# Two loads moved to another queue, copies given a priority, transposes spread and a split begun earlier in a fused hybrid layer

## The chip, the core and the metric

One NeuronCore of a Trainium2 chip runs the whole kernel. TensorE (PE) multiplies matrices into the eight banks of PSUM, VectorE (DVE) and ScalarE (ACT) work elementwise and empty PSUM, GpSimd (POOL) does a little elementwise work and issues some transfers, and SyncE (SP) issues most of the transfers. Each engine, and each queue of transfers, works off its own list of instructions strictly in order: an instruction that waits holds up everything behind it on that engine. The metric is the device time of one execution in microseconds, and less is better.

## The reference, cut to what matters

```python
h = rmsnorm(x) * gain                      # (512, 2048), all in float32
u = h @ w_in                               # 4104 + 4288 + 2 * 2048 columns
u_fox, u_rwkv, g_a, g_b = split(u)
o_a = fox_attention(q, k, v, log_f) * silu(z_a)      # 8 heads of 128
o_b = (groupnorm(rwkv7_scan(...)) + bonus) * silu(z_b)   # 16 heads of 64
m = sigmoid(g_a) * (o_a @ w_proj_fox) + sigmoid(g_b) * (o_b @ w_proj_rwkv)
return rmsnorm(x + m @ w_out) * final_gain
```

The two gates g_a and g_b are products of the normalised input (512 x 2048) with 2048 x 2048 weights each. The merge needs both gates, both branch outputs and the projections.

## The kernel before

**Numbers as pairs.** Every large product is taken in three float32r products: an operand a is split into hi (rounded to float32r) and lo = a - hi, and hi*hi, hi*lo and lo*hi are added in PSUM. So each piece of weights that arrives (`raw`) costs ACT one copy (`whi`, line 267) and DVE one subtraction (`wlo`, line 268) before PE can use it. `next_piece` keeps up to four raw pieces in flight on SP's queue (line 240); a new one can only be issued when `wlo` of an old one is done. It splits pieces up to three ahead, with a priority of 150 (`HW`).

**Who orders what.** The order on PE and SP is the order of the program (`manual_schedule`). ACT, DVE and POOL get their order from a planner that goes by priority and by the times that it expects; `tc.high_priority(offset=...)` raises a priority, 300 for `HP`, 150 for `HW`. The order is fixed before the run.

**Stage 1** (to about 950 us) interleaves the input products of the two branches with the attention heads and the recurrence (`rwkv_front`, `rwkv_back`, `rwkv_chain`). The chain's small copies between its products carry `HP`. The last chain ends with the store of its output to `ob_d` in POOL's queue (line 771).

**The gates** are four half-width products, g = 0 to 3, each taken in seven block products instead of eight (a Strassen scheme). The first of the seven, called c11, is done for all g in a loop of its own (line 1041): 96 products of 128x512 into two PSUM banks for each g, in two halves kb = 0 and 1. After kb = 0 both banks are copied out (`p1`, line 1060) and stored to `p1_d`; after kb = 1 their tanh is taken (line 1064) and stored to `sg_d`. The next half goes into the same banks.

While c11 runs, DVE and ACT build sums of the blocks of the normalised input (`sum_step`: three DVE operations and one ACT copy each, for "d1", "s3", "s2" and "s4", four times each). "d1" lies in the tiles named by eight tags of the attention (`fqh` to `fpT0`), "s2" is wanted by units 6, and "s4" by units 3.

When the last chain is done, `open_late` gives the memory of the recurrence to `gates_rest`, which does the other six products as units (g, p, j): for g = 0 units 5 and 7 alternate for j = 0 to 3, then come four units 6, four units 3 and four units 4. Each unit is 12 PE products. Unit 5 loads weight blocks b11 and b12 and adds them (`X`), unit 7 loads b22 and makes two sums more, unit 6 works on what is left in `X`, and unit 3 on b22 as it is; unit 4 takes `X` after a transfer in POOL's queue has added the missing block to it (line 969). `load(upto)` issues the loads of 512 KB in SP's queue (line 949), one or more units ahead; `prep(n)` makes a unit's operands. At unit (5, 0) of each g the two `p1` tiles are read back (line 991).

**The projections and the merge.** After the gates `branch(0, ob_d)` loads the eight tiles of the recurrence's output and splits them, the first four into the tags of "d1" (line 1099). Two branches (br) by four column blocks (n) by eight pieces (k) of 12 products follow, each n in four banks. In br = 1 the merged tile of block n - 1 is transposed by PE after k = 4 (`turn_merged`, line 1109): four groups of four 128x128 transposes, each group into one bank, emptied by ACT (`mhi`) and DVE (`mlo`). The last of the four comes in the output product, before its ninth piece (kk = 8). The output product then runs to the end.

Of the kernel before, what the change touches and what calls it, by code (L numbers as in the profile page):

```python
# [9 lines left out]
F32 = mybir.dt.float32  # L10
F32R = mybir.dt.float32r
# [6 lines left out]
P = 128  # L18
# [38 lines left out]
def hybrid_layer(  # L57
# [363 lines left out]
    def split(hi, lo, a):  # L421

        S.copy(hi, a)  # L423
        V.tensor_tensor(lo, a, hi.bitcast(F32), ALU.subtract)  # L424
# [430 lines left out]
    def stage1():  # L855
# [40 lines left out]
            return a[:, KB * kb + 2 * j:KB * kb + 2 * j + 2, 256 * th:256 * th + 256]  # L896

        d1 = []

        def sum_step(which, j):  # L900
            two = lambda nm: fox.tile([P, T], F32, tag="fpr", bufs=2, name=f"{nm}_{which}_{j}").rearrange(
                "p (k t) -> p k t", k=2)
            if which == "d1":
                tags = ("fqh", "fql", "fkh", "fkl", "fv", "fz", "fcb", "fpT0")[2 * j:2 * j + 2]
                d1.append([fox.tile([P, T], F32R, tag=t, name=f"d1_{t}").rearrange("p (k t) -> p k t", k=2)
                           for t in tags])
            hl = (hhi, hlo)
            a11, a21, a12, a22 = ([quarter(a, kb, th, j) for a in hl] for kb in range(2) for th in range(2))
            x, y, op, dst = {"d1": (a21, a22, ALU.subtract, d1[j]), "s3": (a11, a21, ALU.subtract, a21),
                             "s2": (d1[j], a11, ALU.subtract, a11), "s4": (a12, a11, ALU.add, a12)}[which]  # L910
            st, su = two("st"), two("su")
            tt(V, st, x[0].bitcast(F32), y[0].bitcast(F32), op)
            tt(V, su, x[1].bitcast(F32), y[1].bitcast(F32), op)
            tt(V, st, st, su, ALU.add)
            split(dst[0], dst[1], st)
# [18 lines left out]
        def gates_rest(wp):  # L934
# [8 lines left out]
            def load(upto):  # L943
                while at[0] < len(loads) and loads[at[0]][0] <= upto:
                    n, b = loads[at[0]]
                    at[0] += 1
                    g, p, j = units[n]
                    t = wp.tile([P, 2, 512], F32, tag=f"b{b}", bufs=3 if b == "22" else 2, name=f"b{b}_{g}{p}{j}")
                    nc.sync.dma_start(t, gate_w(g, int(b[0]) - 1, int(b[1]) - 1, j).rearrange("(k p) m -> p k m", p=P))
                    raw[n, b] = t  # L950

            def prep(n):
# [31 lines left out]
            for n, (g, p, j) in enumerate(units):  # L984
                ready_upto(n + 2)
                load(n + 4)
                if (p, j) == ("5", 0):
                    pz = [ps_mm(f"z5_{g}_{t}") for t in range(2)]
                    p1 = [ev("p1", f"p1_{g}_{t}") for t in range(2)]
                    for t in range(2):  # L990
                        nc.sync.dma_start(p1[t], p1_d[g, t])
                elif (p, j) == ("7", 0):
                    if g % 2:
                        px = [ps_ms(f"x7_{g}"), ps_y(f"y7_{g}")]
                    else:
                        px = [psm.tile([P, T], F32, tag="ch", bufs=2, name=f"x7_{g}_{t}") for t in range(2)]
                elif (p, j) == ("6", 0):
                    py = [ps_ms(f"y6_{g}_{t}") for t in range(2)]
                ps = pz if p in "53" else px if p in "74" else py
                hi, lo = ready.pop(n)  # L1000
                begin, end = p in "576", p in "634"
                for t in range(2):
                    for kk in range(2):
                        k = 2 * j + kk
                        th, kb = {"7": (1, 0), "6": (0, 0), "3": (0, 1), "4": (1, 1)}.get(p, (0, 0))
                        if p == "5":
                            ah, al = (a[:, kk, t * P:(t + 1) * P] for a in d1[j])
                        else:
                            ts = slice(256 * th + t * P, 256 * th + (t + 1) * P)
                            ah, al = (a[:, KB * kb + k, ts] for a in (hhi, hlo))  # L1010
                        for a, w, i in ((ah, hi, 0), (ah, lo, 1), (al, hi, 2)):
                            mm(ps[t], a, w[:, kk, :], start=begin and k == 0 and i == 0,
                               stop=end and k == KB - 1 and i == 2, skip_group_check=True)
                            yield
                    if j < 3:
                        continue
                    if p == "5":
                        p5 = [None, None] if t == 0 else p5
                        p5[t] = ev("p5", f"p5_{g}_{t}")
                        S.copy(p5[t], ps[t])  # L1020
                    elif p == "6":
                        tt(V, p1[t], p1[t], py[t], ALU.add)
                        u3 = ev("u3", f"u3_{g}_{t}")
                        tt(V, u3, p1[t], px[t], ALU.add)
                        tt(V, p5[t], p5[t], u3, ALU.subtract)
                        S.activation(p5[t], p5[t], AF.Tanh, scale=0.5)
                        store_gate(p5[t], g, 1, 1, t)
                    elif p == "3":
                        u3 = ev("u3", f"c12_{g}_{t}")
                        tt(V, u3, pz[t], p1[t], ALU.subtract)  # L1030
                        S.activation(u3, u3, AF.Tanh, scale=0.5)
                        store_gate(u3, g, 0, 1, t)
                    elif p == "4":
                        tt(V, p1[t], p1[t], px[t], ALU.add)
                        S.activation(p1[t], p1[t], AF.Tanh, scale=0.5)
                        store_gate(p1[t], g, 1, 0, t)
                if left and p == "6":
                    sum_step(*left.pop(0))

        rest = []  # L1040
        for g in range(4):
            ps = [ps_mm(f"c11_{g}_{t}") for t in range(2)]
            for kb in range(2):
                for j in range(4):
                    ws = [next_piece(), next_piece()]
                    order = [(kk, t) for kk in range(2) for t in range(2)]
                    if j == 3:
                        order = [(kk, t) for t in range(2) for kk in range(2)]
                    for kk, t in order:
                        k = 2 * j + kk  # L1050
                        ah, al = (a[:, KB * kb + k, t * P:(t + 1) * P] for a in (hhi, hlo))
                        whi, wlo = (w[:, 0, :] for w in ws[kk])
                        for a, w, i in ((ah, whi, 0), (ah, wlo, 1), (al, whi, 2)):
                            mm(ps[t], a, w, start=kb == 0 and k == 0 and i == 0,
                               stop=kb == 1 and k == KB - 1 and i == 2, skip_group_check=True)
                            yield
                        if j == 3 and kk == 1:
                            if kb == 0:
                                p1 = keep.tile([P, T], F32, tag=KEEP[t], name=f"p1_{g}_{t}")
                                S.copy(p1, ps[t])  # L1060
                                G.dma_start(p1_d[g, t], p1)
                            else:
                                sg = keep.tile([P, T], F32, tag=KEEP[2 + t], name=f"c11_{g}_{t}")
                                S.activation(sg, ps[t], AF.Tanh, scale=0.5)
                                store_gate(sg, g, 0, 0, t)
                    if free["fox"] == 7 and first_sums:
                        sum_step(*first_sums.pop(0))
                    if g == 3 and kb == 1 and not first_sums:
                        sum_step("s2", j)
                    open_late()  # L1070
# [16 lines left out]
                nc.sync.dma_start(sg, sg_d[br][t * P:(t + 1) * P, n * 512:(n + 1) * 512])  # L1087
                sgs[br, n, t] = sg

        FT = ("fqh", "fql", "fkh", "fkl", "fv", "fz", "fcb", "fpT0")  # L1090

        def branch(br, src):

            got = []
            for i in range(8):
                o = mg.tile([P, T], F32, tag="oraw", bufs=4, name=f"oraw_{br}_{i}")
                nc.sync.dma_start(o, src[i])
                if i // 4 == br:
# [32 lines left out]
        for br in range(2):  # L1131
            for n in range(4):
                load_gates(br, n)
                pss = four_banks(n, f"p_{br}_{n}")
                for k in range(KB):
                    whi, wlo = next_piece()
                    ohi, olo = both[br][k]
                    for t in range(4):
# [4 lines left out]
                        yield  # L1143
                        mm(pss[t], olo[:, ts], whi[:, 0, :], start=False, stop=(k == KB - 1))
                        yield
                    if br == 1 and n > 0 and k == 4:
                        yield from turn_merged(n - 1)
                    if br == 0 and n == 3 and k == 3:
                        both.append(branch(1, oa_d))
                for t in range(4):  # L1150
# [54 lines left out]
    for n in range(4):  # L1205
        pss = four_banks(n, f"o_{n}")
        for kk in range(KC if n < 3 else KC // 2):
            whi, wlo = next_piece()
            if n == 0 and kk == 8:
                for _ in turn_merged(3):  # L1210
                    pass
            if n == 1 and kk % 2 == 0:
                load_late(KC // 2 + kk // 2)
            for t in range(4):
# [54 lines left out]
```

## Time and profile before

| what | value |
|---|---|
| runs | 1679.1, 1683.52, 1687.18 us; median 1683.52 us |
| the profiled execution | 1678.78 us, of which the span of the trace is 1677.0 us |
| PE busy | 1600.5 us, 95% of the span |
| DVE, ACT, POOL busy | 1128.4 us (67%), 772.5 us (46%), 127.5 us (8%) |
| transfers | 216.39 MB, mean 129 GB/s |
| granted TensorE clock, mean | 0.988 |

The shares of busy time are means over stages; a stage is read from the tables of windows and from the waits. Sums are made against the profiled execution; the median of the runs shown is 4.7 us above it.

### The profile page before, as it was taken

The page shows a single profiled execution, that of the slowest core. Times are in us where ns is not written, and L with a number is a line of the kernel's source. Part 1 is how long each engine was busy: PE and PEld are TensorE (multiplying, and loading weights), DVE is VectorE, ACT ScalarE, POOL GpSimd, SP SyncE. Part 2 cuts the span into 40 slices and gives each one's busy share as a digit, 9 for nine tenths or more (in the row PEclk, how much of TensorE's full clock was granted, in tenths as well). Part 3 has the DMA queues.
Part 4 walks back from the last instruction along what each step waited for, and adds up shares of the span by engine and source line. Part 5 has one row for each costly group of instructions (what it writes and reads, how often), then busy time and mean ns, then how long its engine had stood idle before and what let it go on. Part 6 is the DMA issues. An engine that isn't in the chain of part 4 may idle for free. (4 is left out here: it accounts for less than half of the span.)

```text
span 1677.0 us, 23568 instructions
## 1 busy us (share of the span) xinstructions
PE 1600.5 (95%) x8378; PEld 1303.1 (78%) x8378; DVE 1128.4 (67%) x2173; ACT 772.5 (46%) x1503; POOL 127.5 (8%) x205
## 2 busy tenths in 40 slices
PE   6999899999999999999999898699999999999998
PEld 5888687787787877877878777488888788778886
DVE  6468677786697687776976779977886334544432
ACT  7533545536436446464464376444444322323322
POOL 3000000000000001000010000011111000001110
PEclk9999999999999999999999999799999999999999
DMA  5343234243333342433333467678775545363422
GB/s 166 97 104 93 75 79 111 64 117 86 89 92 95 88 105 76 104 86 92 87 92 94 115 190 218 200 220 218 231 230 149 189 154 171 128 206 127 138 83 100
DMA packets 235756, 216.39 MB, mean 129 GB/s; under 512 B 40326, under 2 KB 174062, under 8 KB 234998
## 3 DMA queue, kind: packets, MB, share of 16 engines
q1 hardware_dynamic: 224582, 183.40, 38.7%
q0 software_dynamic: 9616, 28.34, 6.2%
q10 hardware_dynamic: 1440, 3.15, 0.5%
q8 instruction: 66, 1.08, 0.3%
q14 instruction: 52, 0.43, 0.1%
HBM read 193.84 MB, written 20.99 MB: 128 GB/s over the span
## 5 line engine op out<-in xcount | busy, mean ns | idle before, releaser
L136 PE MATMUL p<-whi_p,o 128*128 128x512 f32 x512 | 161.0, 394 | 2.8 <-ACT o L423 1.9
L136 PEld LDWEIGHTS p<-whi_p,o 128*128 128x128 f32 x512 | 96.1, 188 | 25.6 <-ACT o L423 2.4
L482 DVE TENSOR_TENSOR Wt<-W,Lt 128x16 f32<-128x16 f32 (+30 forms) x248 | 101.6, 410 | 6.2
L268 DVE TENSOR_TENSOR wlo_p<-raw_p,whi_p 128x512 fp32r<-128x512 f32 x64 | 43.5, 691 | 88.6 <-ACT whi_p L267 88.6
L136 PE MATMUL p<-wlo_p,o 128*128 128x512 f32 x256 | 100.8, 394 | 0.4 <-DVE wlo_p L268 0.2
L268 DVE TENSOR_TENSOR wlo_o<-raw_o,whi_o 128x512 fp32r<-128x512 f32 x56 | 42.6, 762 | 81.4 <-ACT whi_o L267 81.1
L267 ACT ACTIVATE whi_p<-raw_p 128x512 fp32r<-128x512 f32 x64 | 40.5, 632 | 115.3 <-PE p L136 42.2
L136 PE MATMUL o<-whi_o,mhi 128*128 128x512 f32 x224 | 87.2, 389 | 0.0
L136 PE MATMUL o<-whi_o,mlo 128*128 128x512 f32 x224 | 87.2, 389 | 0.0
L136 PE MATMUL o<-wlo_o,mhi 128*128 128x512 f32 x224 | 87.2, 389 | 0.0
L423 ACT CAST h<-X 128x1024 fp32r<-128x1024 f32 x48 | 50.5, 1053 | 69.9 <-PE z L136 25.3
L136 PE MATMUL c<-whi_g,hhi 128*128 128x512 f32 x128 | 53.4, 418 | 25.4 <-ACT whi_g L267 16.8
L424 DVE TENSOR_TENSOR l<-X,h 128x1024 fp32r<-128x1024 f32 x48 | 58.7, 1222 | 26.7 <-ACT h L423 26.4
L267 ACT ACTIVATE whi_o<-raw_o 128x512 fp32r<-128x512 f32 x56 | 35.4, 631 | 89.5 <-PE o L136 80.6
L642 DVE TENSOR_REDUCE W<-Wt 128x8 f32<-128x16 f32 (+30 forms) x248 | 72.6, 293 | 5.6
L136 PEld LDWEIGHTS p<-wlo_p,o 128*128 128x128 f32 x256 | 48.1, 188 | 12.2 <-DVE wlo_p L268 1.5
L719 ACT ACTIVATE pre<-SV,E 64x64 f32<-64x64 f32 x112 | 38.6, 345 | 41.0 <-DVE SV L732 40.1
L267 ACT ACTIVATE whi_g<-raw_g 128x512 fp32r<-128x512 f32 x64 | 39.7, 630 | 33.8 <-PE c L136 16.1
L423 ACT CAST h<-b 128x1024 fp32r<-128x1024 f32 x32 | 33.7, 1052 | 46.7 <-PE y L136 24.3
L136 PE MATMUL c<-wlo_g,hhi 128*128 128x512 f32 x128 | 52.5, 410 | 0.8 <-DVE wlo_g L268 0.8
L136 PE MATMUL u_fq<-hhi,whi_fq 128*128 128x512 f32 x128 | 52.4, 409 | 0.0
L136 PE MATMUL u_fq<-hlo,whi_fq 128*128 128x512 f32 x128 | 52.4, 409 | 0.0
(426 smaller groups left out, 4692.5 us busy)
## 6 DMA issues: line engine op xcount, KB each, us to landing
b<-in_w_in_dram SPq DMA_DIRECT2D x64, 512.0 KB
raw_g<-in_w_in_dram SPq DMA_DIRECT2D x64, 256.0 KB
raw_o<-in_w_out_dram SPq DMA_DIRECT2D x56, 256.0 KB
raw_k<-in_w_in_dram SPq DMA_DIRECT2D x32, 256.0 KB
raw_r<-in_w_in_dram SPq DMA_DIRECT2D x32, 256.0 KB
raw_z<-in_w_in_dram SPq DMA_DIRECT2D x32, 256.0 KB
raw_v<-in_w_in_dram SPq DMA_DIRECT2D x32, 256.0 KB
raw_fq<-in_w_in_dram SPq DMA_DIRECT2D x32, 256.0 KB
```

Source lines behind the costliest of these rows:

```text
L136: PE.matmul(out, lhsT=lhsT, rhs=rhs, start=start, stop=stop, **kw)
L267: S.activation(whi, raw, AF.Copy)
L268: V.tensor_tensor(wlo, raw, whi.bitcast(F32), ALU.subtract)
L423: S.copy(hi, a)
L424: V.tensor_tensor(lo, a, hi.bitcast(F32), ALU.subtract)
L482: eng.tensor_tensor(o, a, b, op)
L642: V.tensor_reduce(W[:, :, i], tmp[:, :, 0:i + 1], AX.X, ALU.add)
L719: S.activation(pre[hs[q]], SV[hs[q], c, q, :], AF.Copy, scale=E1[hs[q], c, CH:CH + 1])
```

## The change

1. The first loads of `gates_rest` (units n < 4, six loads of 512 KB) and the two `p1` loads of g = 0 are issued in POOL's queue instead of SP's.
2. The copies and tanh between c11's halves get the priority of the recurrence's chain (`HP`).
3. `turn_merged` is taken one group of four transposes at a time: after k = 3, 4, 5 and 6 in the projections, before kk = 7, 8, 9 and 10 in the output product, instead of four groups at once.
4. The first four tiles of the recurrence's output are loaded and split during the last gates' units (g = 3, units 3 and 4, j = 0 and 2), not after them. Their raw tiles come from the attention's tag `fpr`.

```diff
+        FT = ("fqh", "fql", "fkh", "fkl", "fv", "fz", "fcb", "fpT0")
+        o_first = []
+        def split_o(i, br, src):
+            o = fox.tile([P, T], F32, tag="fpr", bufs=2, name=f"oraw_{br}_{i}")
+            nc.sync.dma_start(o, src[i])
+            hi, lo = (fox.tile([P, T], F32R, tag=FT[2 * i + x], name=f"o{x}_{br}_{i}") for x in range(2))
+            split(hi, lo, o)
+            o_first.append((hi, lo))
...
-                    nc.sync.dma_start(t, gate_w(g, int(b[0]) - 1, int(b[1]) - 1, j).rearrange("(k p) m -> p k m", p=P))
+                    (G if n < 4 else nc.sync).dma_start(
+                        t, gate_w(g, int(b[0]) - 1, int(b[1]) - 1, j).rearrange("(k p) m -> p k m", p=P))
...
-                        nc.sync.dma_start(p1[t], p1_d[g, t])
+                        (G if g == 0 else nc.sync).dma_start(p1[t], p1_d[g, t])
...
+                if g == 3 and p in "34" and j % 2 == 0:
+                    split_o(len(o_first), 0, ob_d)
...
-                                S.copy(p1, ps[t])
+                                with tc.high_priority(offset=HP):
+                                    S.copy(p1, ps[t])
...
-                                S.activation(sg, ps[t], AF.Tanh, scale=0.5)
+                                with tc.high_priority(offset=HP):
+                                    S.activation(sg, ps[t], AF.Tanh, scale=0.5)
...
-            got = []
-            for i in range(8):
+            got = o_first if br == 0 else []
+            for i in range(len(got), 8):
...
-                    if br == 1 and n > 0 and k == 4:
-                        yield from turn_merged(n - 1)
+                    if br == 1 and n > 0 and 2 < k < 7:
+                        if k == 3:
+                            turning = turn_merged(n - 1)
+                        next(turning)
...
-            if n == 0 and kk == 8:
-                for _ in turn_merged(3):
-                    pass
+            if n == 0 and 6 < kk < 11:
+                if kk == 7:
+                    turning = turn_merged(3)
+                next(turning)
```

## Rows read from the trace of the kernel before

**Rows 1.** The page's head: the span, and PE's busy time and instructions.
```profile
span 1677.0 us, 23568 instructions
PE 1600.5 (95%) x8378; PEld 1303.1 (78%) x8378; DVE 1128.4 (67%) x2173; ACT 772.5 (46%) x1503; POOL 127.5 (8%) x205
```

**Rows 2.** PE's waits, whole run: who waited for whom, total us, times, longest.
```profile
PE c L136 <- ACT whi_g L267: 16.8, 2, 15.8
...
PE mT L140 <- DVE mlo L1121: 4.5, 4, 1.7
...
PE z L136 <- DVE l L424: 2.7, 1, 2.7
PE c L136 <- ACT p L1060: 2.4, 3, 1.0
PE p L136 <- ACT o L423: 1.9, 1, 1.9
...
PE c L136 <- ACT c L1064: 1.2, 2, 0.7
...
PE p L136 <- ACT whi_p L267: 0.9, 1, 0.9
```

**Rows 3.** Stages of 20 us: length, busy us by engine, PEclk, DMA share, GB/s.
```profile
1040.00:1060.00 20.00, 4.24 (x20) 3.19 (x18) 18.75 (x27) 7.27 (x11) 1.62 (x3) 0.70 0.25 91
1060.00:1080.00 20.00, 18.94 (x73) 14.77 (x73) 16.99 (x25) 11.22 (x18) 1.08 (x2) 0.88 0.71 221
1080.00:1100.00 20.00, 17.29 (x63) 13.73 (x64) 18.93 (x18) 7.90 (x9) 0.02 (x1) 0.83 0.74 252
```

**Rows 4.** PE in order of time: start, us, [idle before and its releaser].
```profile
1043.74 0.39 PE L136 MATMUL c<-whi_g,hlo 128*128 128x512 f32 x1
1059.90 0.79 PE L136 MATMUL c<-whi_g,hhi 128*128 128x512 f32 x1 [15.76 <-ACT whi_g L267]
...
1063.53 0.63 PE L136 MATMUL c<-whi_g,hhi 128*128 128x512 f32 x1
1063.95 0.63 PE L136 MATMUL c<-wlo_g,hhi 128*128 128x512 f32 x1
```

**Rows 5.** ACT in order of time around the end of PE's longest wait.
```profile
1058.27 1.04 ACT L423 CAST h<-X 128x1024 fp32r<-128x1024 f32 x1 [4.12 <-DVE X L482]
1059.22 0.62 ACT L267 ACTIVATE whi_g<-raw_g 128x512 fp32r<-128x512 f32 x1
```

**Rows 6.** SP's queue in order of time, from several windows.
```profile
1039.72 0.92 SPq L240 DMA_DIRECT2D raw_g<-in_w_in_dram  x2
...
1061.20 2.06 SPq L240 DMA_DIRECT2D raw_g<-in_w_in_dram  x2
...
1071.09 0.93 SPq L949 DMA_DIRECT2D b<-in_w_in_dram  x2
```

**Rows 7.** DVE in order of time: a sum for units 3, two sums of weights.
```profile
1053.52 0.69 DVE L482 TENSOR_TENSOR st_s<-hhi 128x512 f32<-128x512 f32 x1
...
1056.96 1.22 DVE L482 TENSOR_TENSOR X<-b,b 128x1024 f32<-128x1024 f32 x1
...
1080.75 1.23 DVE L482 TENSOR_TENSOR b<-b,b 128x1024 f32<-128x1024 f32 x1 [1.33 <-DMA b<-in_w_in_dram]
```

**Rows 8.** The chain that ended last: start, us, what.
```profile
1072.07 8.59 DMA b<-in_w_in_dram
...
1113.33 10.99 PE z L136 x48
```

**Rows 9.** POOL in order of time, and the issues of line 969 (KB, us to landing).
```profile
1049.63 0.54 POOL L771 DMA_DIRECT2D ob_d<-y  x1 [4.03 <-DVE y L770]
...
1099.98 1.28 POOL L969 DMA_DIRECT2D X<-in_w_in_dram  x1 [24.59 <-DVE l L424]
...
X<-in_w_in_dram POOLq DMA_DIRECT2D x16, 512.0 KB, 6.2
```

**Rows 10.** PE and ACT at one boundary between c11's halves.
```profile
988.54 0.50 PE L136 MATMUL c<-whi_g,hhi 128*128 128x512 f32 x1 [0.93 <-ACT p L1060]
...
1044.17 0.58 ACT L1060 COPY p<-c 128x512 f32<-128x512 f32 x1 [0.77 <-PE c L136]
```

**Rows 11.** SP's queue at the start of the projections.
```profile
1302.75 2.13 SPq L1097 DMA_DIRECT2D oraw<-ob_d  x4
1304.92 2.04 SPq L1087 DMA_DIRECT2D sg<-sg_d  x4
1307.01 3.09 SPq L240 DMA_DIRECT2D raw_p<-in_w_proj_rwkv_dram  x3
```

More of the change, by code (lines that the diff above doesn't have):

```diff
@@ L903, in sum_step @@
             if which == "d1":
-                tags = ("fqh", "fql", "fkh", "fkl", "fv", "fz", "fcb", "fpT0")[2 * j:2 * j + 2]
+                tags = FT[2 * j:2 * j + 2]
                 d1.append([fox.tile([P, T], F32R, tag=t, name=f"d1_{t}").rearrange("p (k t) -> p k t", k=2)
@@ L1088, in load_gates @@
                 sgs[br, n, t] = sg
-        FT = ("fqh", "fql", "fkh", "fkl", "fv", "fz", "fcb", "fpT0")
         def branch(br, src):
-            got = []
-            for i in range(8):
+            got = o_first if br == 0 else []
+            for i in range(len(got), 8):
                 o = mg.tile([P, T], F32, tag="oraw", bufs=4, name=f"oraw_{br}_{i}")
```

## The prediction, made before the run

> **What bounds the kernel now.** I read the page's head first. PE is busy for 1600.5 of 1677.0 us [rows 1], so at most 76.5 us can be won without taking work from PE, and an edit counts only where PE stands idle or runs slowly. PE's waits come next, because each edit should answer to one of them. Four groups do [rows 2]: one wait of 15.8 us for `whi_g` in c11 and one of 2.7 us for a unit's `l` (edit 1), five waits of 3.6 us together for the copies between c11's halves (edit 2), four of 4.5 us in the transposes (edit 3), and two of 2.8 us at the start of the projections (edit 4).
>
> The long wait needs the stages. From 1040 to 1060 us PE works 4.24 us, and over the next 40 us its granted clock is 0.88 and 0.83 [rows 3]. PE ends c11's first half for g = 3 at about 1044 and gets its next operand at 1059.90. Behind that idle time products start 0.42 us apart [rows 4], the lower clock level, where a later run of 48 takes 10.99 us, or 0.229 us each [rows 8], at the full one. From 1043.97 to the first unit 3 at 1113.33 [rows 8] PE has 192 products by the code (48 of c11, 96 of units 5 and 7, 48 of unit 6). At 0.229 us they take 44.0 us and the stage takes 69.4. So 25.4 us are lost here, 15.8 of them in the one wait, and this is what edit 1 is about.
>
> Why was `whi_g` late? SP had issued the raw pieces by about 1040.6 [rows 6], and only 91 GB/s moved from 1040 to 1060 [rows 3]; it was not a transfer. ACT ran `whi_g` at 1059.22, directly after `h<-X` at 1058.27, which had waited 4.12 us for DVE's `X` [rows 5]. DVE began `X` at 1056.96, behind sums that are wanted much later: `st_s<-hhi` at 1053.52 belongs to "s4", for units 3 [rows 7]. So the urgent split stood in ACT's list behind a unit's operand, whose DVE work stood behind sums without haste. The loss is one of order, on engines that are nearly full: DVE works 54.7 of these 60 us [rows 3].
>
> The order also explains the second stop. SP issues its next raw piece only at 1061.20, when `wlo_g` has freed a buffer, and the loads for units n = 2 and 3 stand behind the raw pieces until 1071.09 [rows 6]. Their data is then waited for over 8.59 us [rows 8], DVE takes `b` at 1080.75 [rows 7], and PE waits for `l`.
>
> **The change, part by part.**
>
> *Edit 1, the loads in POOL's queue.* It takes six loads of 512 KB and two of 256 KB from SP and gives them to POOL. POOL needs 1.28 us to issue such a load and it lands 6.2 us later in the median [rows 9]: some 10 us of POOL time, with POOL busy 1.6 of 20 us [rows 3], so the issuing is hidden. Two things follow. The loads of units 2 and 3 no longer stand behind raw pieces that wait for DVE. And the planner no longer expects the raw pieces of c11's second half behind 1.5 MB in SP's queue, so I expect it to put `whi_g` ahead of `h<-X`, and the units' operands ahead of "s4".
>
> What it can give is bounded above by PE: 25.4 us, if nothing else binds. DVE binds sooner. From 1043.2 us it has, by the code, 43 operations of 128x512 (4 to end the chain, 11 left of "s2", 12 for `wlo`, 16 of "s4") and 25 of 128x1024 (20 for units 5 and 7, 4 for units 6, one for the first unit 3). At 0.69 and 1.22 us [rows 7] that is 29.7 + 30.5 = 60.2 us, which ends at 1103.4; PE's units 3 began at 1113.33, so 10 us are won even if all of it must precede them. The last three sums of "s4" (12 x 0.69 = 8.3 us) can run beside units 3: then 18 us. Between the two I take 13, the lower half, since DVE and ACT hand each sum back and forth and DVE was not full before either. What speaks for less: the store of `ob_d` stands in POOL's list at 1049.63 [rows 9]. If the first loads fall behind it, three issues and a landing put `X` at 1050.2 + 3.8 + 6.2 = 1060.2, 3 us later than now. From below edit 1 is worth -3 us.
>
> *A rule against it.* A row shows that the raw pieces were issued in time and that the loads for units 2 and 3 were issued 31 us after their neighbours of line 240 [rows 6]; the queue's order was late, not the engines that move the data. The Trainium skill (DMA: Bandwidth & Descriptors, section "Issuing engines are not separate DMA queues") says that transfers from all queues share the same 16 engines, and that issuing from several only saves the issuing time. By that the edit would be worth about the 0.46 us of issue (0.93 for two) for each of eight loads, 4 us, and the sum below would be 12.5 instead of 21.5.
>
> *Edit 2, the copies' priority.* It adds no instruction. A copy takes 0.58 us, and PE has three products (0.69 us) in the other bank to cover it. At 988.54 PE waited 0.93 us [rows 10]; the five waits are 3.6 us [rows 2]. A copy that starts at once still began some 0.04 us after PE's modelled end and had 0.58 us to run [rows 10], so a few tenths stay each time. I take 2 us, with 0 and 3.6 as bounds; what is displaced on ACT is a `whi_g` with pieces in hand.
>
> *Edit 3, the transposes.* The same 64 transposes, copies and subtractions, but about 2.75 us (12 products) apart. A group needs a free bank, and with two or three banks the previous group has at least 2.75 us for its 0.6 us on ACT and 0.69 on DVE, so all four waits of together 4.5 us [rows 2] should go. Twelve more changes between products and transposes cost an estimated 0.5 us at most. I take 4, with bounds 2.5 and 4.5. Starting one piece earlier costs nothing: the merged block's last sums are over by then.
>
> *Edit 4, the early split.* Four casts, four subtractions and four loads move to 1278 to 1300 us. PE then has ohi and olo for k = 0 to 3 when it gets there (1.9 us saved). The other four tiles' loads, which stood at 1302.75, move up to where the first four were, and `raw_p`, which SP reached at 1307.01 behind them [rows 11], is issued some 5 us earlier, which removes the 0.9 us wait [rows 2]. I take 2.5, with 0 and 2.8 as bounds.
>
> Sum: 13 + 2 + 4 + 2.5 = 21.5 us. From the profiled execution's 1678.78 that is 1657.3; the median of the runs stands 4.74 above it, so I forecast a median of **1662 us**. After 1113 PE is the bound without a gap until the transposes, so nothing takes the gain back.
>
> **The rivals.** Times are against 1683.5.
>
> - *The loads gain no more than their issue.* The planner still puts `whi_g` behind `h<-X`, or "s4" ahead of it; only the second stop shrinks. Edit 1 is worth about 5 us (2.7 of waiting and some of the slow clock), the sum 13.5, the time 1670. For it: DVE is 91% busy here. Against: "s4" need not come first. The Trainium skill's rule on issuing engines (same page and section) leads to the same place.
> - *PE alone binds.* The planner orders everything well: 25 + 3.6 + 4.5 + 2.8 = 36, the time 1647.6. Against it stands DVE's 60 us.
> - *The stall only changes its name.* POOL's store or 3 MB more among c11's raw pieces make them late: edit 1 is worth -3 to 0, the sum 3 to 8 us, the time 1676 to 1680.
> - *Slower: the raised copies block ACT.* The planner places a copy where it expects PE's last product; if PE is later, ACT stands still with `whi_g` behind. ACT already waited 0.77 us so at 1044.17 [rows 10]. Splits run up to three pieces ahead, 6 products each, so 18 x 0.229 = 4.1 us of hold cost nothing; beyond that PE pays one for one. At 8 ends of halves, a hold of 8 us costs 31 us and, with edit 1 then at 13, gives 1693; the forecast's gain is eaten from 6.8 us of hold on. Against it: PE's own delays in c11 are far below that, apart from the long one.
>
> **How the numbers follow.** About 0.5% (8.4 us) is what a measurement of this kernel can tell from no change. Chances: the forecast with edit 1 between 9 and 18 us, 0.45; the loads worth little, 0.22; PE alone, 0.10; the stall renamed, 0.14; slower, 0.09. The first three are faster by over 0.5%: 0.77; the fourth is the same: 0.14; the last slower: 0.09. For 8 in 10 I leave out the slower case, the worse half of the renamed one and the best end of PE alone: 1650 to 1680. The likeliest case's own range is 1655 to 1668.
>
> **What would show it.** Right: `whi_g` for g = 3 within 2 us of PE's end of the first half; PE's granted clock at 1.00 there; units 3 begin some 69 - 13 = 56 us after that end; no wait of `mT` for `mlo`; the first product of the projections without its 1.9 us. Wrong: a wait of over 5 us for `whi_g`, `l` or `X` that stays in this stage, "s4" still ahead of `X` on DVE, POOL's first loads issued after the store of `ob_d`, or ACT idle for PE in front of line 1060 for several us.

## The result, and the profile after

The changed kernel takes 1661.58 us (median of 4 runs, 1661.34 to 1661.74), the kernel before beside it 1682.97 (4 runs, 1679.1 to 1687.18): the ratio is 0.9872, with a 95% interval of 0.9848 to 0.9896. The forecast was 1662. The profiled execution took 1661.46 us; between the two profiled executions lie 17.3 us, between the medians 21.4, since the runs of before scatter over 8 us and its profiled one lies near their low end.

The forecast of the median came out; its terms did not, and the longest wait of before did not go where the prediction sent it. The page's head of the changed kernel, and PE's waits over its whole run (answering [rows 1] and [rows 2]):

```profile
span 1659.7 us, 23572 instructions
...
PE 1600.1 (96%) x8378; PEld 1303.3 (79%) x8378; DVE 1127.0 (68%) x2173; ACT 771.8 (47%) x1503; POOL 132.9 (8%) x213
```

```profile
PE z L136 <- ACT h L423: 11.2, 1, 11.2
...
PE c L136 <- ACT whi_g L267: 2.4, 1, 2.4
...
PE p L136 <- DVE wlo_p L268: 1.1, 3, 0.6
PE z L136 <- DVE l L424: 0.9, 1, 0.9
...
PE c L136 <- ACT c L1079: 0.4, 1, 0.4
```

PE's work is the same 1600 us; only idle time went. The waits of the transposes (`mT`), of the projections' `o` and of the copies `p` are gone, and `whi_g` is down from 16.8 to 2.4 us, of which the 15.8 at the end of c11's first half are gone and the other one, early in c11, has grown from 1.0. A new line leads: 11.2 us of PE's product `z` for `h`, the first unit 5. The stages of 20 us (columns as in [rows 3]) show it as a hole that moved:

```profile
1040.00:1060.00 20.00, 15.00 (x65) 11.75 (x64) 19.90 (x32) 13.02 (x21) 6.13 (x10) 0.99 0.69 214
1060.00:1080.00 20.00, 12.78 (x43) 9.91 (x44) 17.84 (x19) 6.48 (x7) 1.93 (x4) 0.67 0.84 293
1080.00:1100.00 20.00, 20.00 (x89) 16.43 (x88) 19.15 (x21) 10.53 (x12) 4.83 (x4) 1.00 0.74 176
```

Before, the first of these stages was nearly empty and the next two slow; now the first works, the second has the hole, and the third is full. DVE is busy for 56.9 of the 60 us, 2.2 more than in [rows 3]. ACT in order of time (answers [rows 5]) shows why the first stage works: `whi_g` for g = 3 runs at the end of c11's first half, between the two copies, and behind no `h<-X`.

```profile
1042.50 0.59 ACT L1074 COPY p<-c 128x512 f32<-128x512 f32 x1 [0.68 <-PE c L136]
1043.42 0.63 ACT L267 ACTIVATE whi_g<-raw_g 128x512 fp32r<-128x512 f32 x1 [0.33 <-DMA raw_g<-in_w_in_dram]
...
1065.18 1.05 ACT L423 CAST h<-X 128x1024 fp32r<-128x1024 f32 x1 [4.17 <-DVE X L482]
```

POOL's instructions and DVE's (POOL answers [rows 9], DVE [rows 7]) show why the second stage has a hole. POOL reaches the loads at 1056.54, behind the store of `ob_d`, which waited 8.40 us for DVE's `y`, and two stores of gates. It issues six loads in 4.31 us; the first data is there 5.9 us after the first issue, and DVE, which has just finished a sum of "s4", waits 2.13 us more for it.

```profile
1053.78 0.54 POOL L771 DMA_DIRECT2D ob_d<-y  x1 [8.40 <-DVE y L770]
1054.65 0.54 POOL L928 DMA_DIRECT2D sg_d<-c  x1 [0.33 <-ACT c L1079]
1056.01 0.54 POOL L928 DMA_DIRECT2D sg_d<-c  x1 [0.82 <-ACT c L1079]
1056.54 4.31 POOL L959 DMA_DIRECT2D b<-in_w_in_dram  x6
```

```profile
1060.39 0.69 DVE L482 TENSOR_TENSOR st_s<-hhi 128x512 f32<-128x512 f32 x1
...
1063.86 1.23 DVE L482 TENSOR_TENSOR X<-b,b 128x1024 f32<-128x1024 f32 x1 [2.13 <-DMA b<-in_w_in_dram]
```

PE in order of time (answers [rows 4]; the last row is the first unit 3):

```profile
1054.69 0.39 PE L136 MATMUL c<-whi_g,hlo 128*128 128x512 f32 x1
1066.28 0.79 PE L136 MATMUL z<-h,d_fqh 128*128 128x512 f32 x1 [11.20 <-ACT h L423]
...
1072.02 0.63 PE L136 MATMUL z<-l,d_fqh 128*128 128x512 f32 x1
1072.45 0.63 PE L136 MATMUL z<-h,d_fql 128*128 128x512 f32 x1
...
1103.29 0.39 PE L136 MATMUL z<-h,hhi 128*128 128x512 f32 x1
```

The same product in the kernel before (the chain of [rows 8] counts it from 1113.33):

```profile
1113.16 0.39 PE L136 MATMUL z<-h,hhi 128*128 128x512 f32 x1
```

After the hole the first dozen products start 0.43 us apart, the lower clock level, and from 1073 on 0.23 us, without a stop up to the units 3. Before had two stops there, each with its slow products; after has one.

Where the time came from, by the start of the same product before and after: the first unit 3 is 9.9 us earlier (1113.2 and 1103.3), the first projection 11.9 (1302.0 and 1290.1), the first output product 16.5 (1491.7 and 1475.2), the last one 17.3. One microsecond of the first 9.9 was there before c11 began (936.75 and 935.79).

### The profile page after: what moved, and what is told of

Read it like the earlier page. It is cut to its first block, busy times and chain, and to the rows that moved or that the text cites. A ratio compares the mean times of both kernels' runs of the same rounds, so it can differ in the third digit from the quotient of the medians.

```text
span 1659.7 us, 23572 instructions
## 1 busy us (share of the span) xinstructions
PE 1600.1 (96%) x8378; PEld 1303.3 (79%) x8378; DVE 1127.0 (68%) x2173; ACT 771.8 (47%) x1503; POOL 132.9 (8%) x213
## 4 chain that ended last, share of the span: by engine, by line
PE 60%; issue 15%; DVE 12%; DMA 5%; ACT 4%; POOL 2%; SPq 2%; POOLq 0%; ACTq 0%; DVEq 0%
PE o L136 11%; PE p L136 8%; PE u_fq L136 5%; PE u_fk L136 5%; PE c L136 5%; PE u_v L136 4%; PE u_z L136 4%; PE u_fv L136 3%; PE u_fz L136 3%; DVE Wt L482 3%; PE u_k L136 2%; DVE W L642 2%; PE u_r L136 1%; POOL X L980 1%; DMA lora<-in_rwkv_a_dram 1%
## 5 line engine op out<-in xcount | busy, mean ns | idle before, releaser
L136 PEld LDWEIGHTS p<-wlo_p,o 128*128 128x128 f32 x256 | 48.1, 188 | 12.5 <-DVE wlo_p L268 2.1
L423 ACT CAST h<-b 128x1024 fp32r<-128x1024 f32 x32 | 33.7, 1053 | 43.3 <-PE y L136 21.4
L268 DVE TENSOR_TENSOR wlo_g<-raw_g,whi_g 128x512 fp32r<-128x512 f32 x64 | 43.3, 685 | 14.0 <-ACT whi_g L267 13.8
```

The costliest lines, as they stand in the source:

```text
L136: PE.matmul(out, lhsT=lhsT, rhs=rhs, start=start, stop=stop, **kw)
L268: V.tensor_tensor(wlo, raw, whi.bitcast(F32), ALU.subtract)
```

## The experiments

Each run is given with its median, its range and its ratio to the kernel before. The changed kernel itself is 1661.58. The kernel before, measured beside each group of runs, had medians from 1679.5 to 1683.0, so differences of one or two microseconds between groups are not shown by the times alone.

**The four parts, each undone.** In `undo1_loads` all loads are back in SP's queue:

```
-  (G if n < 4 else nc.sync).dma_start(t, gate_w(...))
+  nc.sync.dma_start(t, gate_w(...))
-  (G if g == 0 else nc.sync).dma_start(p1[t], p1_d[g, t])
+  nc.sync.dma_start(p1[t], p1_d[g, t])
```

> The changed kernel with edit 1 undone: the loads of units n < 4 and of p1 for g = 0 are in SP's queue again, edits 2 to 4 stay. Theory (order): the planner sets the split of the second half's first piece behind h<-X again, PE waits for whi_g some 14 to 17 us at the end of c11's first half for g = 3, units 3 begin some 9 to 10 us later than in the changed kernel, and the time is 1661.6 + 10 = 1672 us (1669 to 1676). Rival (the loads only save issuing time): 1664 to 1666 us and no long wait for whi_g. Second rival (edits 2 to 4 are worth little and edit 1 was everything): above 1678 us.

Measured: 1672.02 us (1668.25 to 1674.42), ratio 0.9937 (0.992 to 0.9953). Edit 1 is worth 10.4 us. The first unit 3 begins 13.4 us later than in the changed kernel (1116.7; 9 to 10 were expected), 1.5 of them from before c11. PE's waits over the run have those for `whi_g`, `l` and `h` of before again, somewhat longer:

```profile
PE c L136 <- ACT whi_g L267: 18.6, 2, 16.2
...
PE z L136 <- DVE l L424: 3.3, 1, 3.3
...
PE z L136 <- ACT h L423: 1.2, 1, 1.2
```

In `undo2_priority` the two `with tc.high_priority(offset=HP):` around the copies are gone.

> The changed kernel with edit 2 undone: the copies and the tanh between c11's halves have no raised priority. Theory of the prediction (a saved wait is saved time): 2 us slower, 1663.6 us, with waits of c for lines 1074 and 1079's copies of 2.5 to 3.6 us. Rival, from the changed kernel's trace (a wait for whi_g grew from 1.0 to 2.4 us as those for the copies went): within 1 us of 1661.6 us.

Measured: 1661.43 us (1660.46 to 1661.77), ratio 0.9878 (0.9864 to 0.9893). Edit 2 is worth nothing. Without it the copies' waits are back:

```profile
PE z L136 <- ACT h L423: 10.0, 1, 10.0
...
PE c L136 <- ACT p L1073: 2.9, 4, 1.0
...
PE c L136 <- ACT c L1077: 1.2, 2, 0.7
```

With the priority these 4.1 us are 0.4, but one split of `whi_g` early in c11 is 2.4 us late (0.8 here), with a granted clock of 0.91 from 960 to 980 us where this run has 1.00. The planner's order has changed there: with the priority, an attention instruction (`pr`) that waits 1.64 us for DVE stands ahead of that `whi_g` on ACT (966.49 and 967.11), without it behind (968.62 and 967.68). So c11 from its first product to the start of its last takes 118.9 us with the priority and 119.2 without. An earlier end of c11 would hardly have shown: behind it stands the wait for `h`, 11.2 us with the priority and 10.0 without.

In `undo3_transposes` the merged transposes stand in one block again (`if br == 1 and n > 0 and k == 4: yield from turn_merged(n - 1)`, and the same for the last block).

> The changed kernel with edit 3 undone: four groups of transposes at once. Theory (the four waits of mT for mlo are the whole price): 4.5 to 5.3 us slower, 1666 to 1667 us, and the waits are back with 4.5 us in all. Rival (spreading costs something of its own in changes between products and transposes): 2.5 to 3.5 us slower, 1664 to 1665 us.

Measured: 1668.68 us (1667.08 to 1670.88), ratio 0.9924 (0.991 to 0.9937). The kernel is 7.1 us slower by the medians, 6.6 by the spans, more than either forecast. PE's waits over the run, the lines that are new or longer than in the changed kernel:

```profile
PE mT L140 <- DVE mlo L1134: 4.4, 4, 1.4
...
PE p L136 <- DVE wlo_p L268: 1.4, 2, 1.2
PE p L136 <- ACT whi_p L267: 1.4, 1, 1.4
```

The transposes' own waits are 4.4 us, as in [rows 2]. The rest is not in them: around 1391 us the second branch's first weights come late by 1.4 us, PE's clock falls to 0.91 there, and it does 72 products between 1380 and 1400 us against 83. That this is edit 3's doing isn't shown. The transposes come later, ACT waited for the transfer of these weights, and PE has the same wait of 1.4 us in `late_acc22`, `late_x_first` and `late_x_first_acc22` below, where the transposes are spread as in the changed kernel. ACT here, then PE in `late_acc22`:

```profile
1390.80 2.57 ACT L267 ACTIVATE whi_p<-raw_p 128x512 fp32r<-128x512 f32 x4 [10.86 <-DMA raw_p<-in_w_proj_fox_dram]
```

```profile
1392.81 0.50 PE L136 MATMUL p<-whi_p,o 128*128 128x512 f32 x1 [1.39 <-ACT whi_p L267]
```

What is shown of edit 3 is the 4.4 us; whether it is worth more stays open.

In `undo4_split` the early call of the branch output's split is gone (`if g == 3 and p in "34" and j % 2 == 0: split_o(...)`).

> The changed kernel with edit 4 undone: all eight tiles of the recurrence's output are loaded and split after the gates. Theory: the 1.9 us wait of the first projection's product is back and with it 0.9 us for a late piece of weights, 2.0 to 3 us slower, 1663.6 to 1664.6 us. Rival (the wait moves to the next piece of weights, which comes late in either case): within 1 us of 1661.6 us.

Measured: 1665.26 us (1661.71 to 1671.52), ratio 0.9907 (0.9889 to 0.9924). Edit 4 is worth 3.7 us by the medians, with a wide scatter, and 3.2 by the spans. The wait of 1.9 us for `o` is back, that of 0.9 for a piece of weights is not, and the stage behind it runs at a clock of 0.91 where the changed kernel has 20.00 us of work at 1.00:

```profile
1280.00:1300.00 20.00, 18.05 (x73) 14.39 (x72) 9.40 (x13) 8.63 (x14) 2.15 (x4) 0.91 0.54 180
```

By the medians the four parts sum to 10.4 + 0 + 7.1 + 3.7 = 21.2 us, and the whole is 21.4. That they meet so closely is chance: by the ratios, which differ from the changed kernel's by 0.0065, 0.0006, 0.0052 and 0.0035, the parts sum to 27 us, and edit 3's part holds the late weights.

**What of edit 1 does it.** `pool_units23` gives POOL only the loads that stood behind the raw pieces, those of units n = 2 and 3, and `p1`: `(G if 1 < n < 4 else nc.sync)`.

> The changed kernel, but of the six first loads only the three of units 2 and 3 (and p1 of g = 0) are issued in POOL's queue; the three of units 0 and 1 are in SP's again, ahead of the raw pieces of c11's second half. Theory (the order that the planner writes): whi_g of that half stands behind h<-X again and PE waits 14 to 17 us for it; only the second stop shrinks: 1666 to 1669 us. Rival (what cost time was that loads stood behind raw pieces that wait for DVE): the long wait is gone, 1661 to 1663 us.

Measured: 1664.09 us (1663.08 to 1667.06), ratio 0.9897 (0.988 to 0.9914). PE has one idle stretch of over half a microsecond in this stage, and it is the one of before in place and length:

```profile
1059.78 0.79 PE L136 MATMUL c<-whi_g,hhi 128*128 128x512 f32 x1 [16.23 <-ACT whi_g L267]
```

The order was as the theory had it: with units 0 and 1 in SP's queue ahead of the raw pieces, `whi_g` stays behind `h<-X` (1058.14 and 1059.10 on ACT). Its price was not. The kernel with the whole 16 us wait is only 2.5 us slower than the changed one by the medians (the intervals of the ratios overlap), and 7.9 faster than `undo1_loads` (they don't). So some three quarters of edit 1 is the second stop: POOL issues these loads at 1050.95 where SP did at 1071.09 [rows 6], and PE runs from 1061 to the units 3 (1105.9) without waiting for an operand. From its return to the units 3 it takes 46.1 us here and took 53.3 before: 7.1 us for a stop whose waits are 2.7 and 0.5 us in the trace, most of the rest being 13 products 0.43 us apart behind the longer one.

`late_in_sp` asks whether POOL's queue is needed: all loads in SP's queue again, but opened later, behind the last raw pieces of c11.

```
+  if g == 3 and kb == 1 and j >= 1:
       open_late()
```

> Edit 1 in another way: all loads stay in SP's queue, none in POOL's, but gates_rest is opened only after the second pair of pieces of c11's second half for g = 3, so that its first loads stand behind the last raw pieces of c11 and are issued at about 1047 instead of 1056 us. Theory (order): no long wait for whi_g without POOL's help, and since DVE has s2 and the first s4 in front of X, X begins at about 1061 and the wait of z for h stays at 8 to 10 us: 1659 to 1662 us. Rival (the changed kernel's 11.2 us wait is because POOL issues the loads late): data at 1055, a wait of about 3 us, 1652 to 1655 us. Second rival (POOL's queue is what brings the gain): 1670 us or more.

Measured: 1660.59 us (1658.82 to 1662.61), ratio 0.9874 (0.9858 to 0.9891). It isn't. SP issues the first loads at 1049.30, 7 us earlier than POOL in the changed kernel, and DVE still takes `X` at 1062.29, 1.6 us earlier and now without waiting for data: it is at other sums until then. SP's queue, then DVE:

```profile
1049.30 1.45 SPq L959 DMA_DIRECT2D b<-in_w_in_dram  x3
```

```profile
1061.68 0.69 DVE L482 TENSOR_TENSOR st_s<-st_s,su_s 128x512 f32<-128x512 f32 x1
1062.29 1.22 DVE L482 TENSOR_TENSOR X<-b,b 128x1024 f32<-128x1024 f32 x1
1063.42 0.68 DVE L424 TENSOR_TENSOR hlo<-st_s,hhi 128x512 fp32r<-128x512 f32 x1
```

**Is DVE the bound?** `late_no_s4` is `late_in_sp` without the sums "s4" (`left = []`): it leaves out these four sums, and the units 3 multiply the block of the normalised input as it is, so that it computes other gates.

> The version with the late loads in SP's queue, with the four sums s4 left out (units 3 multiply the block as it is), which takes 16 operations of 0.6 us each from DVE. Theory (DVE is the bound from c11's end to the first units 3): z's wait loses another 2 to 3 us and the time falls by 3 to 6 us against the version with the sums, 1654 to 1658 us. Rival (the loads, or PE, set the time): within 1.5 us of the version with the sums.

Measured: 1658.09 us (1655.77 to 1659.67), ratio 0.9862 (0.9843 to 0.9881): 2.5 us less by the medians, 4.8 by the spans. `X` is at 1058.90 and the units 3 begin at 1099.1, 4.5 us earlier. DVE's work counts, but taking 11 us of it (16 operations of 0.69) gives back less than half; by the medians the gain lies between theory and rival, and the intervals of the ratios overlap.

`late_s4_pool` keeps "s4" and puts three of the four operations of each on POOL (`E = G if which == "s4" else V`).

> The version with the late loads in SP's queue, with three of the four elementwise operations of each s4 on POOL, 12 of some 1.5 us each (what POOL took for this shape elsewhere in the kernel), 18 us of POOL in all. Theory (DVE is the bound): at most 2 us slower than the version without s4, 1655 to 1660 us. Rival (POOL and DVE slow each other, or POOL's transfers for units 4 come late behind the sums): no faster than the version with the sums on DVE, 1660 us or more.

Measured: 1672.05 us (1671.01 to 1673.46), ratio 0.9942 (0.9929 to 0.9955): 11.5 us worse than `late_in_sp`. POOL in order of time, then DVE:

```profile
1061.55 1.26 POOL L482 TENSOR_TENSOR st_s<-st_s,su_s 128x512 f32<-128x512 f32 x1
...
1064.79 2.18 POOL L482 TENSOR_TENSOR su_s<-hlo 128x512 f32<-128x512 f32 x1 [0.63 <-DVE hlo L424]
1067.04 2.13 POOL L482 TENSOR_TENSOR st_s<-st_s,su_s 128x512 f32<-128x512 f32 x1
```

```profile
1064.63 1.21 DVE L482 TENSOR_TENSOR b<-b,b 128x1024 f32<-128x1024 f32 x1
1065.77 2.28 DVE L424 TENSOR_TENSOR l<-X,h 128x1024 fp32r<-128x1024 f32 x1
1067.97 1.76 DVE L268 TENSOR_TENSOR wlo_p<-raw_p,whi_p 128x512 fp32r<-128x512 f32 x1
```

An operation that takes 1.21 us on DVE takes 2.28 while POOL adds, one of 0.69 takes 1.76, and POOL's take 2.1 instead of 1.26: each waits for the other. From 1060 us to the units 3 DVE is busy for 42.45 us in this kernel and in `late_in_sp`, with 35 operations here and 48 there. The Trainium skill (SBUF — State Buffer, section "SBUF: two separate sides") says that GpSimd and a VectorE operation with two inputs in SBUF share one pair of ports, which the first holds for its whole instruction; these rows agree.

The ports are not the whole price. In ACT's list the cast of a sum of "s4" stands ahead of the first unit's operand:

```profile
1062.85 0.62 ACT L423 CAST hhi<-st_s 128x512 fp32r<-128x512 f32 x1 [4.96 <-POOL st_s L482]
1063.37 1.04 ACT L423 CAST h<-X 128x1024 fp32r<-128x1024 f32 x1
```

DVE had begun `X` at 1059.14, 3.2 us earlier than in `late_in_sp`, but PE's first product of unit 5 comes only 0.2 us earlier (1064.46 and 1064.69). Up to the units 3 ACT waits 21.0 us for POOL's sums in four such casts. How the 11.5 us divide between the ports and this order no run shows.

**Two limits close together.** `late_acc22` takes 4.6 us from DVE behind the first operand: four of the sums `X + b22` become accumulating loads in POOL's queue.

```
   if p == "7":
+      if g == 0:
+          G.dma_start(xs[j], gate_w(g, 1, 1, j)..., accum_op=ALU.add)
```

> As late_in_sp (all loads in SP's queue, opened late; 1660.6 us), but for g = 0 the four sums X + b22 of DVE (128x1024, 1.22 us each) are made by accumulating loads in POOL's queue, as X + b21 already is. Theory (DVE's work sets when units 3 begin): 4 x 1.14 = 4.6 us leave DVE ahead of units 3, which begin 3 to 4.5 us earlier (1099 to 1100.5), and the time is 1656 to 1658. Rival (the transfers, 2 MB more in this stretch, or POOL's issues bound it): units 3 at 1103 or later, a wait for X or b grows, the time is 1660 to 1664.

Measured: 1659.58 us (1658.74 to 1662.64), ratio 0.9871 (0.9853 to 0.9889): no change. DVE now idles (16.17 of 20 us between 1080 and 1100, where `late_in_sp` has 19.84), and the first unit 3 stays at 1103.3. The theory that the whole of DVE's work sets it fell here. What stayed is the time of the first operand:

```profile
1064.30 0.79 PE L136 MATMUL z<-h,d_fqh 128*128 128x512 f32 x1 [8.47 <-ACT h L423]
```

From there PE has 144 products, 33.0 us at 0.229, and takes 39.0: 2.7 us are two waits for `l`, the rest its slow start. Behind that product little but PE's own speed is left.

`late_acc22_12` also makes `X = b11 + b12` by an accumulating load.

> As late_acc22, and X = b11 + b12 of g = 0 is made the same way: b11 is loaded into X and b12 accumulated there from POOL's queue, which takes four more sums of 1.22 us from DVE and moves 2 MB more. Theory (DVE alone): another 4.6 us, units 3 at 1095 to 1097, the time 1652 to 1655. Rival (the operand of the first unit 5 now waits for a load, POOL's store of ob_d and an accumulating load one after the other, some 3 to 10 us): PE's wait in front of the first unit 5 grows and the time is 1658 to 1668.

Measured: 1672.67 us (1670.22 to 1673.55), ratio 0.9941 (0.9925 to 0.9958). The rival has the mechanism, and the time lies above even its range: two transfers one after the other, and POOL's queue, cost more than the sum. The first product of unit 5 waits 12.5 us, later ones again, and the units 3 begin at 1116.1.

`late_x_first` leaves DVE all its work and changes its order: the sums "s2" for j = 2 and 3 are made to follow the operands of the first two units, and each "s4" an operand of units 6. A copy of one column that reads that operand (0.15 us) forces it.

```
 def sum_step(which, j, after=None):
     ...
+    if after is not None:
+        V.tensor_copy(st[:, 0, 0:1], after[:, 0, 0:1].bitcast(F32))
```

> As late_in_sp (1660.6 us; X at 1062.29, first unit 5 with a wait of 8.5 us, units 3 at 1103.6), but the sums s2 for j = 2 and 3 follow the operands of the first two units on DVE, and each s4 follows an operand of units 6 (a copy of 128x1 that reads the operand forces the order; no sum is left out). Theory now (the end of c11's last product to the first unit's operand is the price, and PE runs without a gap from there): X waits only for its load, issued at 1049.3 and landed some 6 to 8 us later, so X at 1055.5 to 1057.5 instead of 1062.3, the first product of unit 5 about 5 us earlier, units 3 at 1097.5 to 1100, the time 1654 to 1657. Rival (the whole sum of DVE's work up to units 3 is the price): the sums come back between the later units, PE waits there for l and h, units 3 at 1102 to 1104, the time 1659 to 1662.

Measured: 1662.17 us (1658.18 to 1663.64), ratio 0.9887 (0.9869 to 0.9906): no gain, the rival's time. Yet the first operand came 6.6 us earlier. PE's waits in order of time:

```profile
1058.13 0.51 PE L136 MATMUL z<-h,d_fqh 128*128 128x512 f32 x1 [1.62 <-ACT h L423]
...
1068.14 0.69 PE L136 MATMUL z<-h,d_fkh 128*128 128x512 f32 x1 [3.18 <-ACT h L423]
...
1109.76 0.50 PE L136 MATMUL z<-l,hhi 128*128 128x512 f32 x1 [1.89 <-DVE l L424]
```

The wait of 8.5 us has become seven smaller ones (10.3 us together, with those for `l`), the last of them among the units 3, where DVE does the sums that were put off.

`late_x_first_acc22` does both.

> As late_x_first, and X + b22 of g = 0 by accumulating loads in POOL's queue (as in late_acc22), which takes 4.6 us from DVE between the units. If only the first operand is the price: as late_x_first, 1654 to 1657. If the sums that were moved back make DVE the bound behind the first unit: some 3 to 4 us less than late_x_first, whatever that gives.

Measured: 1657.26 us (1656.67 to 1658.99), ratio 0.9864 (0.9848 to 0.9881). Its first product of unit 5 is at 1055.19, the first unit 3 at 1097.9, 5.4 us earlier than in the changed kernel. So both expectations hold at once: the time is in the range given for the first operand alone, and it is `late_x_first`'s less 4.9 us (3 to 4 were expected), so DVE is the bound once the order is mended, while the same 4.6 us of DVE's work were worth nothing behind a late first operand. It is the lowest time of a kernel that leaves nothing out, 4.3 us below the changed kernel; by the ratios, whose intervals overlap, it is 1.3, and the two can't be told apart with certainty.

The traces can be compared over one stretch that leaves out what differs before and behind it, from c11's first product to the first projection. The changed kernel, then `late_x_first_acc22`:

```profile
935.79 0.39 PE L136 MATMUL c<-whi_g,hhi 128*128 128x512 f32 x1
...
1290.11 0.39 PE L136 MATMUL p<-whi_p,o 128*128 128x512 f32 x1
```

```profile
935.84 0.39 PE L136 MATMUL c<-whi_g,hhi 128*128 128x512 f32 x1
...
1285.09 0.39 PE L136 MATMUL p<-whi_p,o 128*128 128x512 f32 x1
```

It takes 354.3 and 349.3 us in these two, and 353.2 in `late_in_sp`, 354.0 in `late_acc22`, 353.9 in `late_x_first`; each is one execution. Either change alone gives nothing, both together 3.9 us against `late_in_sp`.

## Why the prediction was right, point by point

**The sum** was 21.5 us and the medians moved by 21.4, by luck in two ways. Its errors cancelled: by the medians of the undone kernels edit 1 was 2.6 us too high and edit 2 was 2 too high, edit 3 was 3.1 and edit 4 1.2 too low. And the sum was made against the profiled execution, where 17.3 us came: 1661.46 and not 1657.3. The 4.74 us that the median of before stood above its profiled execution made up for it, but they were scatter of that kernel; the changed one's median stands 0.1 us above its own.

**Edit 1: the order right, what it is worth mostly wrong.** 13 us were forecast and 10.4 measured, within the bounds of DVE (10 to 18). `whi_g` did move ahead of `h<-X`, as said, and units 3 begin 59.6 us after the end of c11's first half (1043.7 by the trace), not 56. But the prediction laid the loss to the long wait. That wait only became shorter and changed its operand, from 15.8 us for `whi_g` to 11.2 us for `h`, and `pool_units23` prices that move at 2.5 us by the medians. The 7.9 us that remain are the second stop, which the rival "no more than their issue" sized at 5 in all; the rival "the stall only changes its name" had what became of the long wait, but not the gain beside it.

Of the prediction's four signs of being wrong three came: a wait of over 5 us (for `h`, made from `X`), "s4" still ahead of `X` on DVE (1060.39), and POOL's loads behind the store of `ob_d`. The step that failed is the one from PE's 25.4 us straight to DVE's total of 60.2 us: between them lies the arrival of the first unit's operand, and no term asked when that would come. The sentence on the store of `ob_d` did ask, and its sign of "less" came true, with `X` at 1063.86 and not 1060.2, since the store itself was issued 4 us later than in [rows 9] and two more stood behind it. That X came 7 us later than before cost little, because c11's second half no longer stood behind it: `late_x_first` has `X` at 1055.61, 8 us earlier than the changed kernel, and no lower time. The 8.59 us which the prediction calls waited for are the transfer's own time on the chain [rows 8]; DVE stood idle 1.33 us for it [rows 7].

That DVE's 60.2 us put the units 3 at 1103.4 and they began at 1103.29 is partly luck. `late_acc22` and `late_x_first` show two limits at nearly the same place, the first operand and the sum of DVE's work: lifting one alone gives nothing, lifting both some 4 us. The durations of 0.69 and 1.22 us also overlap: in `late_in_sp` DVE starts its next operation after 0.61 and 1.13 (1061.68, 1062.29, 1063.42). By these steps the 68 operations would take an estimated 54 us, so waits and operations that the sum left out made up the rest. The reason for taking more than DVE's 10 us, that the last three sums of "s4" run beside the units 3, held only for the last operation of the last sum.

**The granted clock** was to be 1.00 after the first half: it was 0.99 from 1040 to 1060 and 0.67 in the next stage, where PE stood idle for 11.2 us.

**The rule on issuing engines** (the Trainium skill, DMA: Bandwidth & Descriptors, section "Issuing engines are not separate DMA queues") would have put edit 1 at 4 us. The trace agrees with it in that POOL's queue was nothing that SP could not give: `late_in_sp` is as fast. It doesn't show the 4 us: what stands behind waiting pieces in one queue, and what the planner expects of it, was worth 10.4.

**Edit 2: mis-sized, 2 us and then 0.** The copies' waits fell from 3.6 to 0.4 us, more than forecast, and the lower bound was what counted. The step that failed is the one that costed what is displaced on ACT, "a `whi_g` with pieces in hand", at nothing: one split early in c11 came to stand behind an attention instruction, and its wait went from 1.0 to 2.4 us. The rival that it slows the kernel was wrong: ACT waited for PE in front of a copy or tanh for at most 0.8 us, not 8.

**Edit 3: mechanism right, 4 us forecast.** All four waits of the transposes went, 4.4 us by the trace. The 0.5 us allowed for more changes between products and transposes don't show: by the traces four groups lengthen PE's row by 1.8 us when spread (0.44 each, as from 1414.34 to 1415.01) and by 2.1, their wait not counted, in a block of the kernel before (1429.15 to 1433.19). The other 2 to 3 us of the 7.1 measured are the weights of the second branch, for which the prediction had no term and which edit 3 isn't shown to move.

**Edit 4: mechanism right, 2.5 us and then 3.7.** The wait went and SP came to `raw_p` at 1288.15, 2 us before the first projection product and not 5 behind it as in [rows 11]. What the term left out is the clock of the stage behind the wait (0.91 where the wait stands).

## What to carry to other kernels

A wait's length in the trace is not its price: ask what the late operand's engine does next and when the operand after it can come, since a wait that is removed can reappear one operand later (15.8 us became 11.2, worth 2.5), while a short second stop with slow products behind it can be worth twice its wait. When an engine is nearly full, look at its order and its total together: here either alone gave nothing, both together some 4 us by the traces. Here a load's place in a queue mattered more than whose queue it was. And a total that meets the forecast says little of its terms: undo each part.

## What the runs showed of the hardware

- Short stops of PE can cost more than their length: waits of 0.5 and 2.7 us, with 13 products at the lower clock level (0.43 us apart) behind the longer one, made a stage 7.1 us longer (46.1 and 53.3). Not each does: behind a wait of 1.4 us the clock of the stage was 0.91 in `undo3_transposes` and 1.00 in `late_acc22`.
- POOL and DVE adding in SBUF at the same time is worse than DVE alone: 1.21 us became 2.28 and 1.26 became 2.1, and 12 operations given to POOL cost the kernel 11.5 us, a part of it by the order on ACT.
- POOL issued six plain loads of 512 KB in 4.31 us, 0.72 each, where an accumulating one takes it 1.28 [rows 9]; the prediction used the latter for both.
